# A hybrid attention layer with split fp32r products: mask, adaLN, second norm and tail loads rearranged

## The chip, the core and the metric

The kernel runs on one core of a Trainium2 chip. The core has a matrix engine (TensorE, PE), a vector engine (VectorE, DVE), a scalar engine (ScalarE, ACT), a small general engine (GpSimd, POOL) and a queue engine that issues transfers (SyncE, SP). Each runs its own instructions in order and waits for the others by semaphores. PE sums into PSUM, in banks of 512 f32 columns; everything else lies in SBUF. The metric is the device time of one execution in microseconds (us), lower is better.

## What is computed

One decoder layer for 256 tokens (T = 2 halves of 128) of width 2048, all in f32, weights 300 MB in all. The conditioning vector c gives six adaLN vectors of 2048. Cut to what matters here:

```python
mod = silu(c) @ w_ada + b_ada
shift_a, scale_a, gate_a, shift_f, scale_f, gate_f = split(mod, 6)
h = rms_norm(x, g_attn_pre) * (1 + scale_a) + shift_a
proj = h @ w_in                        # 8 differential heads, 8 sparse heads, 16 indexers
diff = softmax(q1 k1^T / 8, causal) - lam * softmax(q2 k2^T / 8, causal)   # per head, then @ v
sparse = softmax(q k^T / sqrt(128), only the 64 keys that the indexer picked)  # then @ v
mixed = concat(norm(diff @ v), sparse @ v) @ w_o
x = x + gate_a * rms_norm(mixed, g_attn_post)
h = rms_norm(x, g_ffn_pre) * (1 + scale_f) + shift_f
ff = (silu(h @ w_gate) * (h @ w_up)) @ w_down
x = x + gate_f * rms_norm(ff, g_ffn_post)
```

## The kernel before

**Products.** A full-precision product is made of three fp32r products of the halves of its operands (`mm3`: hi by hi L192, hi by lo L195, lo by hi L196). `wload` fetches a 1 MB piece of a weight (four k-slices of 512 columns) into one of six `raw` buffers; ACT rounds it to `whi` (L179) and DVE subtracts to get `wlo` (L180), in pieces of 128x1024 with three buffers each. Activations are kept as two halves of the same kind (`h`, `gT`, `mixT`, and `H2` for the FFN).

**adaLN.** `ada_block` makes a vector piece from w_ada, in units of 1 MB (four k-slices of 512 columns). With `on_pe` each slice is one product with c as the fixed operand, 32 columns wide, and four of these lie side by side on the array (L236, tile `ad`). Without it DVE does one multiply-add per slice into `aacc` (L244). `ada_cols` turns a finished row into columns of `modA` or `modF`, with two columns of `sel` for a PE block (L293) or with `ones` per accumulator for a DVE block (L297). modF (scale_f and shift_f) has four blocks of 512; F_DVE names those that DVE takes. Units are used one after the other by `ada_step`, which `side()` calls behind each w_o load and the FFN's first stage at a rate FRATE.

**Stages.** The input projection (about 35 to 390 us), with attention in steps among its products (to 440); w_o (to 503); FFN (508 to 1253); output. Three PSUM banks (`tr_bank`) serve all transposes, score products and small results, four (`mm_bank`) the large sums.

**Attention.** `to_T` transposes q and k (L410) and ACT copies them out (L413). `scores` (L490) puts two softmaxes into two banks, each with a 128-column segment (the first 128 queries) and a 256-column one. `softmax_parts` lets DVE scale, add the mask and take the row extreme in one custom step into SBUF (L501), and ACT takes exp from SBUF (L505). Then come the weighted sum, transposes (L513, L515) and the products with v.

**End of w_o.** `tail_pair` sums the last two column blocks (ci 2 and 3). All loads but the last two are used for both token halves at once. The last two (one per block, one of them in `xhi`/`xlo`) are used for t = 0 first and then for t = 1, 24 products each, so that `residual(0)` runs beside t = 1. `residual` squares the sum on ACT (L783), multiplies by Ga on DVE (L784), gets the row factor ry, makes x1 = x1 + y ry (L859), squares x1 on ACT (L861), gets its row factor r1 on POOL and dg, the diagonal matrix of r1 (L864). `h2_tiles` transposes x1 through dg on PE (L846), and `make_h` (L347 on ACT, L348 on DVE, L350) shifts, scales and splits it into `H2`; `first_half` does the first 8 of 16 k-slices.

**FFN.** With only those 8 slices made, the first NSPLIT column blocks of gate and up are half-summed and copied to `part` (L903), while `ada_step` gets the rest of modF; then the other 8 slices follow, and DVE adds the two halves. `tail_pair` ends w_down in the same manner as w_o, and `out_block` (L972) writes the output.

**Order.** The instructions of an engine are put in order by a scheduler at build time, which works from dependences and modelled times; `keep_in_program_order` pins a few. The order is fixed when the kernel runs.

```python
blocks = [(a, ci) for a in range(0, nk - 4, 4) for ci in cs]
...
tl = {ci: wload(rows, kbase + nk - 4, 4, ci * 512, 512, ph2 if ci == cs[1] else None)
      for ci in cs}
for t in range(T):
    for ci in cs:
        ...
    done[0](t)
```

## Time and profile before

| | before |
|---|---|
| three runs, us | 1262.14, 1262.45, 1264.23 |
| profiled execution, us | 1263.92 |
| its span, us | 1262.1 |
| PE busy | 1230.5 us (97%) |
| DVE busy | 763.6 us (60%) |
| ACT busy | 573.1 us (45%) |
| POOL busy | 23.2 us (2%) |
| HBM read | 307.05 MB |

The span runs from the first instruction to the last; 1.8 us of the profiled execution lie around it. Busy times of different engines lie beside one another and cannot be added. PE's records overlap one another, so a record's length is not what it costs: the distance between starts is. The chain of waits is followed back from the last instruction, and "idle ... <-X" names what released an instruction that had to wait.

### The profile page before, as it was taken

What the parts mean: (1) busy time and instruction counts of PE and PEld (TensorE: products, weight loads), DVE (VectorE), ACT (ScalarE), POOL (GpSimd) and SP (SyncE); (2) the same over time, 40 slices, a digit from 0 to 9 for tenths busy, and PEclk for the clock granted to TensorE, in tenths of its full rate; (3) what the DMA queues carried; (4) which work ended last, traced back from release to release, by engine and by line L of the source; (5) the groups of instructions that cost most, each with busy time, mean ns of one, the idle gap of its engine ahead of it and who ended that gap; (6) DMA issues with size and microseconds to landing.
All of it is one profiled execution on the core that took longest, in us unless ns stands there. A gap on an engine that the chain in (4) does not pass through costs nothing.

```text
span 1262.1 us, 15223 instructions
## 1 busy us (share of the span) xinstructions
PE 1230.5 (97%) x5912; PEld 948.6 (75%) x5912; DVE 763.6 (60%) x1155; ACT 573.1 (45%) x838; POOL 23.2 (2%) x63
## 2 busy tenths in 40 slices
PE   5999999999999999899999999999999999999997
PEld 4666675777656877788888888888888888888885
...
GB/s 382 388 358 334 371 357 204 370 258 272 200 304 266 150 366 279 267 190 322 314 278 262 179 192 241 255 172 195 199 177 192 200 191 185 193 198 182 185 134 67
DMA packets 44713, 310.14 MB, mean 246 GB/s; under 512 B 5848, under 2 KB 5848, under 8 KB 7648
## 3 DMA queue, kind: packets, MB, share of 16 engines
...
q10 hardware_dynamic: 272, 0.00, 0.0%
HBM read 307.05 MB, written 2.10 MB: 245 GB/s over the span
## 4 chain that ended last, share of the span: by engine, by line
PE 93%; DMA 2%; ACT 2%; DVE 1%; issue 1%; POOL 0%; SPq 0%; DVEq 0%; POOLq 0%
PE mm L195 27%; PE mm L192 27%; PE mm L196 27%; PE ad L236 5%; DMA raw<-in_w_ada_dram 1%; PE tr L490 1%; DMA raw<-in_w_in_dram 1%; PE tr L429 1%; PE tr L934 1%; PE tr L410 1%; PE tr L846 1%; PE tr L312 1%; DVE wlo L180 0%; PE tr L293 0%; PE tr L513 0%
## 5 line engine op out<-in xcount | busy, mean ns | idle before, releaser
L180 DVE TENSOR_TENSOR wlo<-raw,whi 128x1024 fp32r<-128x1024 f32 (+1 forms) x383 | 463.4, 1213 | 369.0 <-ACT whi L179 368.2
L179 ACT ACTIVATE whi<-raw 128x1024 fp32r<-128x1024 f32 (+1 forms) x383 | 401.0, 1051 | 519.5 <-PE mm L196 488.6
L195 PE MATMUL mm<-wlo,h 128*128 128x512 f32 (+1 forms) x1056 | 415.1, 393 | 0.8 <-DVE wlo L180 0.8
L196 PE MATMUL mm<-whi,h 128*128 128x512 f32 (+1 forms) x1056 | 410.9, 389 | 1.6 <-DVE h L350 1.6
L192 PE MATMUL mm<-whi,h 128*128 128x512 f32 (+1 forms) x1056 | 380.1, 393 | 1.9 <-ACT whi L179 1.0
L192 PEld LDWEIGHTS mm<-whi,h 128*128 128x128 f32 x1056 | 196.7, 188 | 63.3 <-issue 13.4
L195 PEld LDWEIGHTS mm<-wlo,h 128*128 128x128 f32 x1056 | 198.6, 188 | 60.3 <-issue 10.8
L196 PEld LDWEIGHTS mm<-whi,h 128*128 128x128 f32 x1056 | 198.6, 188 | 42.3 <-DVE h L350 2.1
L195 PE MATMUL mm<-wlo,gT 128*128 128x512 f32 x348 | 135.8, 390 | 0.0
L196 PE MATMUL mm<-whi,gT 128*128 128x512 f32 x348 | 135.4, 389 | 0.0
L192 PE MATMUL mm<-whi,gT 128*128 128x512 f32 x348 | 123.0, 390 | 0.0
L244 DVE SCALAR_TENSOR_TENSOR aacc<-raw,csil,aacc 128x512 f32<-128x512 f32 x126 | 94.0, 747 | 8.0 <-DMA raw<-in_w_ada_dram 5.3
L236 PE MATMUL ad<-raw,c 128*32 128x512 f32 (+2 forms) x640 | 82.8, 523 | 12.8 <-DMA raw<-in_w_ada_dram 12.8
L748 DVE TENSOR_TENSOR PR<-mm,PR 128x512 f32<-128x512 f32 (+1 forms) x88 | 57.0, 669 | 34.2 <-PE mm L196 34.0
L196 PEld LDWEIGHTS mm<-whi,gT 128*128 128x128 f32 x348 | 65.3, 188 | 13.9 <-issue 0.2
L195 PEld LDWEIGHTS mm<-wlo,gT 128*128 128x128 f32 x348 | 65.3, 188 | 13.6 <-issue 0.2
L192 PEld LDWEIGHTS mm<-whi,gT 128*128 128x128 f32 x348 | 65.3, 188 | 13.5
L195 PE MATMUL mm<-wlo,mixT 128*128 128x512 f32 x124 | 49.9, 402 | 0.0
L236 PEld LDWEIGHTS ad<-raw,c 128*32 128x32 f32 x640 | 17.9, 111 | 41.6 <-issue 26.7
L192 PE MATMUL mm<-whi,mixT 128*128 128x512 f32 x124 | 47.6, 402 | 0.7 <-ACT mixT L603 0.7
L196 PE MATMUL mm<-whi,mixT 128*128 128x512 f32 x124 | 45.9, 394 | 0.0
L195 PEld LDWEIGHTS mm<-wlo,mixT 128*128 128x128 f32 x124 | 23.3, 188 | 8.4 <-issue 1.7
(192 smaller groups left out, 673.2 us busy)
## 6 DMA issues: line engine op xcount, KB each, us to landing
raw<-in_w_ada_dram SPq DMA_DIRECT2D x96, 1024.0 KB, 7.2
raw<-in_w_gate_dram SPq DMA_DIRECT2D x44, 1024.0 KB, 5.0
raw<-in_w_up_dram SPq DMA_DIRECT2D x44, 1024.0 KB, 5.0
raw<-in_w_down_dram SPq DMA_DIRECT2D x44, 1024.0 KB, 4.9
raw<-in_w_in_dram SPq DMA_DIRECT2D x39, 1024.0 KB, 7.1
raw<-in_w_o_dram SPq DMA_DIRECT2D x16, 1024.0 KB, 7.0
xs<-in_x_dram SPq DMA_DIRECT2D x2, 1024.0 KB, 6.9
x<-in_x_dram SPq DMA_DIRECT2D x2, 1024.0 KB
```

The source lines that it names most:

```text
L179: made = [ACT.activation(hv, src, AF.Copy), DVE.tensor_tensor(lv, src, hv.bitcast(F32), op=ALU.subtract)]
L180: DVE.tensor_tensor(lv, src, hv.bitcast(F32), op=ALU.subtract)]
L192: i = PE.matmul(ps, lhsT=hi, rhs=whi, start=start, stop=False)
L195: PE.matmul(ps, lhsT=hi, rhs=wlo, start=False, stop=False)
L196: PE.matmul(ps, lhsT=lo, rhs=whi, start=False, stop=stop)
L236: PE.matmul(st["ps"][32 * j:32 * j + 32, :n], lhsT=c33[:, k, 1 - b:33 - b], rhs=w, start=(b == 0 and k < 4), stop=(b == nb - 1 and k >= 12 ...
L244: DVE.scalar_tensor_tensor(acc, w, csil[:, k:k + 1], acc, op0=ALU.mult, op1=ALU.add)
L312: PE.matmul(ps, lhsT=ones, rhs=accs[0], start=True, stop=True)
L410: PE.transpose(tr[:, i * P:(i + 1) * P], PR[:, t, c0:c0 + P], ident)
L429: PE.matmul(sc[i][:, SEG[t]], lhsT=st["q"][r, (2 * j + t) * P:(2 * j + t + 1) * P], rhs=ikT[r, :P * (t + 1)], start=True, stop=True)
L490: PE.matmul(sc[i][:, SEG[t]], lhsT=l, rhs=r, start=True, stop=True)
L748: DVE.tensor_tensor(dst, banks[c0][t][:, :n], dst, op=ALU.add)
```

## The change

Six things change.

1. The mask M is bf16, and so is nselb, the mask of picked keys. `score_banks` first multiplies an identity (`identb`) by the mask into the bank, 128x384, and the score products add to it. q is scaled when it is copied out of the transpose. DVE takes the negated row maximum straight from the bank, and ACT takes exp straight from the bank too.
2. F_DVE is (2, 3): the fourth block of modF goes to DVE.
3. Four column blocks of gate and up are half-summed instead of two (NSPLIT), with `ada_step` at half the rate (FRATE), and `side()` stops two units into modF's second half (SIDE). The partial sums lie in what y, Ga and xhi/xlo held; Gf is loaded and multiplied by its gate later.
4. `post_attn` and `residual` get the second norm from three means, of the square of the sum, of y x1, and of y squared (`st3`), with the mean square of x (`msx`): the mean square of the new x1 is msx + 2 ry mean(y x1) + ry^2 mean(y^2). x1 itself is no longer squared.
5. `tail_pair` keeps the last three loads instead of two for t = 0 and then t = 1, 36 products each, in w_o and in w_down; two of them lie in xhi/xlo and in the upper half of H2.
6. `h2_tiles` makes k-slices in pairs: one half of the pair from DVE, one from ACT, then one rounding copy and one subtraction for both.

```diff
-F_DVE = (2,)
+F_DVE = (2, 3)
...
-FRATE = 2
+FRATE = 1
...
-NSPLIT = 2
+NSPLIT = 4
+SIDE = 2
...
+    identb = ct([P, P], "identb", BF16)
+    DVE.tensor_copy(identb, ident)
+    M = ct([P, 384], "mask", BF16)
...
+    msx = ct([P, T], "msx")
+    DVE.tensor_scalar(msx, ssx, 1.0 / D, EPS, op0=ALU.mult, op1=ALU.add)
...
+        if ns:
+            ACT.activation(o[:, :ns * P], tr[:, :ns * P], AF.Copy, scale=scale)
+        if ns * P < n:
+            ACT.activation(o[:, ns * P:n], tr[:, ns * P:n], AF.Copy)
...
-    def scores(mms):
+    def score_banks(mask, mms):
 
         sc = [tr_bank() for _ in range(2)]
+        for i in range(2):
+            PE.matmul(sc[i][:, :384], lhsT=identb, rhs=mask, start=True, stop=False)
         for t in range(T):
             for i in range(2):
                 l, r = mms(i, t)
-                PE.matmul(sc[i][:, SEG[t]], lhsT=l, rhs=r, start=True, stop=True)
+                PE.matmul(sc[i][:, SEG[t]], lhsT=l, rhs=r, start=False, stop=(t == T - 1))
...
-                DVE.tensor_tensor_reduce(out=s[:, i, SEG[t]], in0=sc[i][:, SEG[t]], in1=mask[:, SEG[t]],
-                                         scale=-scale, scalar=2.0 ** 120, op0=ALU.add, op1=ALU.min,
-                                         accum_out=mn[:, i, t:t + 1])
+                DVE.tensor_reduce(mx[:, i, t:t + 1], sc[i][:, SEG[t]], axis=AX.X, op=ALU.max,
+                                  negate=True)
             for t in range(T):
-                ACT.activation(s[:, i, SEG[t]], s[:, i, SEG[t]], AF.Exp, scale=-1.0,
-                               bias=mn[:, i, t:t + 1], accum_out=l[:, i, t:t + 1])
+                ACT.activation(s[:, i, SEG[t]], sc[i][:, SEG[t]], AF.Exp, bias=mx[:, i, t:t + 1],
+                               accum_out=l[:, i, t:t + 1])
...
+            st["q"] = to_T([(0, c0), (1, c0), (0, c0 + P), (1, c0 + P)], 128 ** -0.5, 4)
...
+    def post_attn(bank, t, ci):
+
+
+        cs_ = slice(ci * 512, ci * 512 + 512)
+        j = tr_bank()
+        ACT.activation(j, bank, AF.Square, scale=D ** -0.5, accum_out=st3[:, t, 0, ci:ci + 1])
+        DVE.tensor_tensor(y[:, t, cs_], bank, Ga[:, cs_], op=ALU.mult)
+        j2 = ph2.tile([P, 512], F32, tag="sil", name=nm("j2"), bufs=3)
+        DVE.tensor_tensor_reduce(out=j2, in0=y[:, t, cs_], in1=x1[:, t, cs_], scale=2.0 / D, scalar=0.0,
+                                 op0=ALU.mult, op1=ALU.add, accum_out=st3[:, t, 1, ci:ci + 1])
+        ACT.activation(j, y[:, t, cs_], AF.Square, scale=D ** -0.5, accum_out=st3[:, t, 2, ci:ci + 1])
...
-        blocks = [(a, ci) for a in range(0, nk - 4, 4) for ci in cs]
-        for a, ci in blocks:
+        blocks = [(a, ci) for a in range(0, nk, 4) for ci in cs]
+        for a, ci in blocks[:-3]:
             for (k, _), (whi, wlo) in wload(rows, kbase + a, 4, ci * 512, 512).items():
                 for t in range(T):
                     mm3(banks[ci, t], *L(k - kbase), t, whi, wlo, k == kbase, False)
             side()
-        tl = {ci: wload(rows, kbase + nk - 4, 4, ci * 512, 512, ph2 if ci == cs[1] else None)
-              for ci in cs}
+
+        spare = [tuple(ph2.tile([P, 1024], F32R, tag=tag, name=nm(tag)) for tag in ("xhi", "xlo"))]
+        spare += [tuple(H2[:, i, k:k + 4, :].rearrange("p k q -> p (k q)") for i in range(2)) for k in (8, 12)]
+        homes = (None, (None, spare[0]), spare[1:])
+        tl = [(ci, wload(rows, kbase + a, 4, ci * 512, 512, homes[i])) for i, (a, ci) in enumerate(blocks[-3:])]
         for t in range(T):
-            for ci in cs:
-                for (k, _), (whi, wlo) in tl[ci].items():
+            for ci, ws in tl:
...
+        if used[0] < need_f1 + SIDE:
+            ada_step(1)
...
+            for i in range(0, 4, 2):
+                hf = wp.tile([P, S], F32, tag="hf", name=nm("hf"), bufs=2)
+                for j in range(2):
+                    src, kk = tr[:, (i + j) * P:(i + j + 1) * P], k + i + j
+                    sc, sh = modF[:, 1, kk:kk + 1], modF[:, 0, kk:kk + 1]
+                    if j:
+                        ACT.activation(hf[:, P:], src, AF.Identity, bias=sh, scale=sc)
+                    else:
+                        DVE.tensor_scalar(hf[:, :P], src, sc, sh, op0=ALU.mult, op1=ALU.add)
+                hi, lo = (H2[:, h, k + i:k + i + 2, qs] for h in range(2))
+                hv = hf.rearrange("p (k q) -> p k q", k=2)
+                ACT.activation(hi, hv, AF.Copy)
+                DVE.tensor_tensor(lo, hv, hi.bitcast(F32), op=ALU.subtract)
...
-            post(banks[ci, t], t, ci, Ga, ssy, y)
-        DVE.tensor_reduce(sst[:, t:t + 1], ssy[:, t], axis=AX.X, op=ALU.add)
-        rstd(ry[:, t:t + 1], sst[:, t:t + 1], 1, D)
+            post_attn(banks[ci, t], t, ci)
+        DVE.tensor_reduce(mean[:, t], st3[:, t], axis=AX.X, op=ALU.add)
+        rt = ry[:, t:t + 1]
+        POOL.tensor_tensor(rt, mean[:, t, 0:1], nhalf[:, 0:1], op=ALU.pow)
+        m = mean[:, t, 1:2]
+        DVE.scalar_tensor_tensor(m, mean[:, t, 2:3], rt, m, op0=ALU.mult, op1=ALU.add)
+        tc.keep_in_program_order(
+            DVE.scalar_tensor_tensor(m, m, rt, msx[:, t:t + 1], op0=ALU.mult, op1=ALU.add))
+        POOL.tensor_tensor(r1[:, t:t + 1], m, nhalf[:, 0:1], op=ALU.pow)
+        POOL.tensor_scalar(dg[t], ident, r1[:, t:t + 1], None, op0=ALU.mult)
         for h in range(2):
             hs = slice(1024 * h, 1024 * h + 1024)
-            DVE.scalar_tensor_tensor(x1[:, t, hs], y[:, t, hs], ry[:, t:t + 1], x1[:, t, hs],
-                                     op0=ALU.mult, op1=ALU.add)
-            ACT.activation(y[:, t, hs], x1[:, t, hs], AF.Square, accum_out=ss1[:, t, h:h + 1])
-        POOL.tensor_tensor(sss[:, t:t + 1], ss1[:, t, 0:1], ss1[:, t, 1:2], op=ALU.add)
-        rstd(r1[:, t:t + 1], sss[:, t:t + 1], 1, D, POOL)
-        POOL.tensor_scalar(dg[t], ident, r1[:, t:t + 1], None, op0=ALU.mult)
+            tc.keep_in_program_order(
+                DVE.scalar_tensor_tensor(x1[:, t, hs], y[:, t, hs], rt, x1[:, t, hs], op0=ALU.mult, op1=ALU.add))
...
+            part = ph2.tile([P, 8, 512], F32, tag="y", name="part")
+            part2 = big.tile([P, 4, 512], F32, tag="Ga", name="part2")
+            part3 = [ph2.tile([P, T, 512], F32, tag=tag, name="part3" + tag) for tag in ("xhi", "xlo")]
+
+            def part_of(lc, wi, t):
+                if lc < 2:
+                    return part[:, 4 * lc + 2 * wi + t, :]
+                if lc == 2:
+                    return part2[:, 2 * wi + t, :]
+                return part3[wi][:, t, :]
...
+            if fc == NSPLIT - 1:
+                Gf = big.tile([P, D], F32, tag="Ga", name="Gf")
+                tc.keep_in_program_order(SP.dma_start(Gf, g_ffn_post[0].partition_broadcast(P)))
+                for b in range(4):
+                    ada_gate(Gf, 5, b * 512, False)
```

On PE in attention, at the second pair of sparse heads (`tr` are the shared PSUM banks, `skT` and `qT` transposed keys and queries, `s` the weighted probabilities, `on` a differential head's output). Before:

```order
L513 MATMUL tr_3286<-ident,s_3188 128x128
L490 MATMUL tr_3292<-skT,qT_3204 128x128
L490 MATMUL tr_3293<-skT,qT_3204 128x128
L490 MATMUL tr_3292<-skT,qT_3204 128x256
L490 MATMUL tr_3293<-skT,qT_3204 128x256
L513 MATMUL tr_3286<-ident,s_3188 128x128 x2
L410 MATMUL tr_3309<-ident,PR 128x128 x4
L602 MATMUL tr_3362<-ident,on_3269 128x128 x2
```

After:

```order
L527 MATMUL tr_3318<-ident,s_3220 128x128
L502 LDWEIGHTS identb
L502 MATMUL tr_3324<-nselb,identb 128x384
L502 LDWEIGHTS identb
L502 MATMUL tr_3325<-nselb,identb 128x384
L506 MATMUL tr_3324<-skT,qT_3236 128x128
L506 MATMUL tr_3325<-skT,qT_3236 128x128
L506 MATMUL tr_3324<-skT,qT_3236 128x256
L506 MATMUL tr_3325<-skT,qT_3236 128x256
L527 MATMUL tr_3318<-ident,s_3220 128x128 x2
L421 MATMUL tr_3343<-ident,PR 128x128 x4
L617 MATMUL tr_3395<-ident,on_3301 128x128 x2
```

Two products of the mask with their weight loads now stand ahead of the score products; the rows behind them are the same.

On PE at the end of w_o (`mm_3876` and `mm_3920` are the last sums, of token half 1; `dg` products make the transposed x1; `ad` is adaLN). Before:

```order
L192 MATMUL mm_3876<-xhi_4146,mixT_1559 128x512
L195 MATMUL mm_3876<-xlo_4147,mixT_1559 128x512
L196 MATMUL mm_3876<-xhi_4146,mixT_1560 128x512
L236 MATMUL ad_4123<-raw_4366,c_105 32x512 x4
L236 MATMUL ad_4123<-raw_4372,c_105 32x512 x4
L236 MATMUL ad_4123<-raw_4412,c_105 32x512 x4
L236 MATMUL ad_4123<-raw_4418,c_105 32x512 x4
L846 MATMUL tr_4236<-dg_3871,x_3850 128x128 x4
L846 MATMUL tr_4257<-dg_3871,x_3850 128x128 x4
L192 MATMUL mm_4326<-whi_4330,h_3866 128x512
```

After:

```order
L195 MATMUL mm_3920<-h_3911,mixT_1567 128x512
L198 MATMUL mm_3920<-h_3911,mixT_1567 128x512
L199 MATMUL mm_3920<-h_3911,mixT_1568 128x512
L877 MATMUL tr_4229<-dg_3915,x_3883 128x128 x4
L877 MATMUL tr_4244<-dg_3915,x_3883 128x128 x4
L195 MATMUL mm_4296<-whi_4300,h_3911 128x512
L198 MATMUL mm_4296<-wlo_4301,h_3911 128x512
```

The sixteen adaLN products between the last w_o product and the dg products are gone. The last products of half 1 read weights from H2's place.

On DVE at the same place (`wlo_4331` and `wlo_4301` are the first FFN weights). Before:

```order
L180 TENSOR_TENSOR wlo_4143<-raw_4140,whi_4142 128x1024
L784 TENSOR_TENSOR y<-mm_3873,Ga 128x512
L784 TENSOR_TENSOR y<-mm_3875,Ga 128x512
L855 TENSOR_REDUCE sst<-ssy 128x1
L155 TENSOR_SCALAR rs_4181<-sst 128x1
L859 SCALAR_TENSOR_TENSOR x_3850<-y,ry,x_3850 128x1024 x2
L180 TENSOR_TENSOR wlo_4331<-raw_4328,whi_4330 128x1024
L784 TENSOR_TENSOR y<-mm_3874,Ga 128x512
```

After (ISA with `j` and `st` is the summed product of y and x1, the next ISA reads its sum out):

```order
L247 SCALAR_TENSOR_TENSOR aacc_4416<-raw_4421,csil,aacc_4416 128x512
L806 TENSOR_TENSOR y<-mm_3919,Ga 128x512
L247 SCALAR_TENSOR_TENSOR aacc_4416<-raw_4421,csil,aacc_4416 128x512
L808 ISA j_4162,st_121<-y,x_3883 128x512
L808 ISA st_121 128x1
L183 TENSOR_TENSOR wlo_4301<-raw_4298,whi_4300 128x1024
L897 TENSOR_REDUCE mean<-st_121 128x3
L183 TENSOR_TENSOR wlo_4305<-raw_4298,whi_4304 128x1024
L901 SCALAR_TENSOR_TENSOR mean<-mean,ry 128x1
L183 TENSOR_TENSOR wlo_4341<-raw_4338,whi_4340 128x1024
L903 SCALAR_TENSOR_TENSOR mean<-mean,ry,msx 128x1
L909 SCALAR_TENSOR_TENSOR x_3883<-y,ry,x_3883 128x1024 x2
```

Between half 0's sums and its x1 stand adaLN multiply-adds and three wlo steps, where before only the norm's own steps stood.

## Rows read from the trace of the kernel before

**Rows 1.** The page: share of the chain that ended last, by engine.

```profile
PE 93%; DMA 2%; ACT 2%; DVE 1%; issue 1%; POOL 0%; SPq 0%; DVEq 0%; POOLq 0%
```

**Rows 2.** Stretches of 50 us: length, then busy us (instructions) per engine, clock, DMA.

```profile
400.00:450.00 50.00, 46.83 (x260) 38.94 (x259) 32.21 (x75) 33.91 (x89) 2.73 (x4) 1.00 0.53 188
...
1000.00:1050.00 50.00, 50.00 (x222) 41.40 (x221) 24.46 (x22) 20.03 (x19) 0.00 (x0) 1.00 0.56 191
```

**Rows 3.** Timeline of PE in the FFN: start us, length us.

```profile
599.62 0.39 PE L192 MATMUL mm<-whi,h 128*128 128x512 f32 x1
599.85 0.39 PE L195 MATMUL mm<-wlo,h 128*128 128x512 f32 x1
```

**Rows 4.** adaLN: PE's groups by shape, then two steps of the chain.

```profile
L236 PE MATMUL ad<-raw,c 128*32 128x512 f32 x448 | 73.0, 603 | 0.0
...
470.12 0.98 PE ad L236 x2
...
521.27 0.79 PE tr L293 x8
```

**Rows 5.** Small products: timeline of a 336-column sum, and a plain f32 group.

```profile
64.75 0.32 PE L195 MATMUL mm<-wlo,h 128*128 128x336 f32 x1
64.90 0.32 PE L196 MATMUL mm<-whi,h 128*128 128x336 f32 x1
...
L312 PE MATMUL tr<-aacc,ones 128*128 128x512 f32 x16 | 8.2, 592 | 0.0
```

**Rows 6.** Softmax steps of DVE and ACT by shape, and one stretch.

```profile
L501 DVE CUSTOM_DVE_ANT_0 s<-tr,mask 128x256 f32<-128x256 f32 x16 | 6.7, 418 | 0.0
...
L505 ACT ACTIVATE s<-s,mx 128x256 f32<-128x256 f32 x24 | 11.9, 497 | 0.0
...
L505 ACT ACTIVATE s<-s,mx 128x128 f32<-128x128 f32 x24 | 9.5, 396 | 10.2 <-DVE mx L501 10.2
...
405.00:415.00 10.00, 8.36 (x49) 6.72 (x50) 8.29 (x27) 7.92 (x30) 1.39 (x2) 1.00 0.82 288
```

**Rows 7.** Timeline of PE at the end of w_o.

```profile
503.31 3.64 PE L236 MATMUL ad<-raw,c 128*32 128x512 f32 x32
508.25 2.05 PE L846 MATMUL tr<-dg,x 128*128 128x128 f32 x16 [1.30 <-POOL dg L864]
...
512.41 0.50 PE L196 MATMUL mm<-whi,h 128*128 128x512 f32 x1 [1.65 <-DVE h L350]
513.84 0.79 PE L192 MATMUL mm<-whi,h 128*128 128x512 f32 x1 [0.93 <-ACT h L345]
514.43 0.63 PE L195 MATMUL mm<-wlo,h 128*128 128x512 f32 x1
514.86 0.63 PE L196 MATMUL mm<-whi,h 128*128 128x512 f32 x1
```

**Rows 8.** The stretch of 10 us around it.

```profile
510.00:520.00 10.00, 7.43 (x35) 5.84 (x34) 5.83 (x16) 7.27 (x19) 1.67 (x4) 0.83 1.01 427
```

**Rows 9.** Timelines of DVE, ACT and POOL at the end of w_o.

```profile
498.70 0.69 DVE L784 TENSOR_TENSOR y<-mm,Ga 128x512 f32<-128x512 f32 x1 [4.43 <-ACT tr L783]
...
502.70 1.22 DVE L180 TENSOR_TENSOR wlo<-raw,whi 128x1024 fp32r<-128x1024 f32 x1
...
502.23 1.05 ACT L861 ACTIVATE y<-x 128x1024 f32<-128x1024 f32 x1
...
507.58 0.62 POOL L864 TENSOR_SCALAR dg<-ident,r 128x128 f32<-128x128 f32 x1
```

**Rows 10.** A stretch behind the half-summed blocks of before.

```profile
590.00:600.00 10.00, 10.00 (x50) 8.38 (x49) 9.89 (x13) 4.65 (x7) 0.00 (x0) 1.00 0.88 313
```

**Rows 11.** Timeline of DVE at the end.

```profile
1252.73 0.74 DVE L972 SCALAR_TENSOR_TENSOR ff<-mm,ry,x 128x512 f32<-128x512 f32 x1
```

**Rows 12.** DMA issues: count, size, median us from issue to landing.

```profile
raw<-in_w_o_dram SPq DMA_DIRECT2D x16, 1024.0 KB, 7.0
...
Gf<-in_g_ffn_post_dram SPq DMA_DIRECT2D x1, 1024.0 KB, 14.6
```

More of the change, by code (lines that the diff above doesn't have):

```diff
@@ L169, in wload @@
                 w = min(step, n - b)
-                if more is not None and a + m == nk:
-                    hi = more.tile([P, 1024], F32R, tag="xhi", name=nm("xhi"))
-                    lo = more.tile([P, 1024], F32R, tag="xlo", name=nm("xlo"))
+                home = more[a // 2] if more else None
+                if home is not None:
+                    hi, lo = home
                 else:
@@ L389, in layer @@
     nsel = pp.tile([P, 384], F32, tag="nsel", name="nsel")
+    nselb = pp.tile([P, 384], BF16, tag="nselb", name="nselb")
     iwS = pp.tile([P, T, 16], F32, tag="iwS", name="iwS")
@@ L476, in tail @@
             DVE.tensor_tensor(nsel, nsel, score, op=ALU.is_equal)
-            DVE.tensor_scalar(nsel, nsel, NEG, None, op0=ALU.mult)
+            DVE.tensor_scalar(nselb, nsel, NEG, None, op0=ALU.mult)
         return [head] + [lambda r=r: rounds(r) for r in range(0, TOPK // 8, 2)] + [tail]
@@ L523, in s0 @@
         def s0():
[L524 removed]
+            st["q"] = to_T([(0, c0), (1, c0), (0, c0 + P), (1, c0 + P)], 128 ** -0.5, 4)
         def s1():
             qT = st["q"]
[L528 to L529 removed]
+            sc = score_banks(nselb, lambda i, t: (qT[:, (2 * i + t) * P:(2 * i + t + 1) * P],
+                                                  skT[:, :P * (t + 1)]))
+            st["s"], st["l"] = softmax_parts(sc)
         def s2():
@@ L847, in h2_tiles @@
                           rhs=dg[t], start=True, stop=True)
-            for i in range(4):
-                make_h(H2, tr[:, i * P:(i + 1) * P], modF, k + i, slice(t * P, (t + 1) * P),
-                       on_act=i % 2 == 1)
+            for i in range(0, 4, 2):
[11 more added lines that the diff above has]
+                DVE.tensor_tensor(lo, hv, hi.bitcast(F32), op=ALU.subtract)
@@ L906, in layer @@
                 h2_tiles(t, 8, 16)
-            for b in range(4):
-                ada_gate(Gf, 5, b * 512, False)
         for lc in range(ng):
+            if fc == NSPLIT - 1:
[3 more added lines that the diff above has]
+                    ada_gate(Gf, 5, b * 512, False)
             c0 = fc * 512
```

39 lines of the change are left out of this document (16 added, 23 removed).

## The prediction

> **What bounds the kernel now.** I read the page's chain of waits first: 93% of the chain that ended last is TensorE (PE) itself [rows 1]. So a change here is worth what it adds to or takes from PE's own queue, plus what it does to the few places where PE stands. The stretches of 50 us say where those are: the FFN shows 50.00 of 50 in every row, at clock 1.00; attention lacks 3.2 us in 400 to 450 [rows 2]. The PE timeline gives the true price of a product: a 128x512 record is 0.39 us long, but the next starts 0.23 us later (0.2265 over many) [rows 3]. All sums below go by such starts. In the FFN the number of products is unchanged and VectorE (DVE) and ScalarE (ACT) have slack [rows 2], so nothing is to be had there but the adaLN products. Three things are left: adaLN products, mask products, and the seam between w_o and the FFN.
>
> **1. The fourth quarter of modF leaves PE.** The 512-column adaLN products hold PE for 73.0 us in 448 records [rows 4], two records to a product: 224 products. F_DVE = (2, 3) makes that 192. Four neighbours run at once on four column tiles, so what costs is the run, not the product: a run of 2 records takes 0.98 us, as one of 8 does [rows 4]. Counting runs in the two orders (one run is up to four products in a row) gives 71 before and 59 after. The block's own work before is five short runs (some 0.98 each, 4.9) and one long one of 3.64 us just behind w_o [rows 7]: 8.6 us. The other three runs go because the rows that stay are cut up less. 12 x 0.98 = **-11.8 us**; at least -8.6, at most -12.5 (a change-over saved with some of them).
> What takes its place: DVE gets 30 more multiply-adds of 128x512 in the half-summed FFN blocks, where PE's products need only the raw weights' two halves. With one unit per two weight steps I lay out some 75 us of DVE work in the 87 us of those blocks. Before, the stage after the first two blocks had DVE at 9.89 of 10 us and PE at 10.00 of 10 [rows 10]: that load is hidden, so I take **0**. If the cover were gone, the overhang would be of the order of those 9 to 12 us (rival E). The block's finish costs 8 more tiny products with ones and 4 fewer with sel; eight records with sel take 0.79 us [rows 4]: **+0.6**, from +0.3 to +1.
>
> **2. Mask by product, exp out of PSUM.** 24 products of 128x384 in bf16 come in (16 with M, 8 with nselb), each with its own weight load. The trace has no bf16 product. From below: a 336-column fp32r product starts 0.15 us after the one before it [rows 5], so 384 columns at that pace are 0.177. From above: a product in plain f32 is two records, and 16 records of 512 columns held PE for 8.2 us [rows 5], 0.51 each; two of 384 columns are at most 0.77. The fp32r row is nearest, since it too goes through once; with some change-over, 0.20 each: 24 x 0.20 = **+4.8**, from +3.7 to +18. The Trainium skill ("TensorE: Matmul & The Clock Gate", Part 1) measures bf16 products at columns / 2.4 GHz plus 2.5 ns; by that, an estimate, the term would be 24 x 0.1625 = 3.9.
> The custom add-and-min on DVE (0.418 us for 256 columns [rows 6]) becomes a maximum of about that size: nothing on PE's path. What does move is when the bank comes free. Before, it was free when DVE had read it; now it is free only when ACT has done both exps from it, 0.50 + 0.40 = 0.9 us later [rows 6]. Three banks serve all transposes and scores. In the order, nine or ten places hand a bank from the scores to a transpose within a few rows (the DSA pairs and the last differential heads); elsewhere 4 or more long products stand between. Attention already lacks 1.64 us of 10 at 405 to 415 [rows 6]. I take two full holds exposed, **+2**, from 0 to +6. The Trainium skill ("PSUM — Partial Sum Buffer", "PSUM bank collisions raise a hardware error") wants two engines kept off one bank at once, reads included; it speaks against this part, since the maximum and the exp now share a bank. By that rule the first exp waits for both maxima and each hold grows by up to 0.42, so two holds would make 2.6 instead of 2.
>
> **3. The seam.** Before: after the last w_o product PE does 3.64 us of adaLN, then stands 1.30 us for dg, 1.65 and 0.93 us for the h pieces, with two short slots between, and then runs at 0.43 us a product instead of 0.23 [rows 7]: the granted clock was 0.83 over 510 to 520 [rows 8], some 3.4 us at the lower level (1.2 GHz) after those idle stretches. Idle 3.9, slow products about 1.2, change-overs and slow transposes 0.8: 5.9 us lost.
> After: the last three loads instead of two close the sums, so token half 1 has 36 products behind half 0, 8.15 us instead of 5.44 (24). The adaLN run is gone. In its place the norm of half 0 has no longer to wait for x1: four squares (1.05 us each [rows 9]) and the sum of two go. Its chain is square, y, product with x1, square of y, mean, power, two tiny steps, power, dg. With 0.69 for y and as much for the product, under 0.8 for a square (that of twice the columns took 1.05), 0.62 for dg and about as much for a power [rows 9], and 0.5 for the tiny steps, that is some 5.3 us; but DVE runs in order, and four adaLN steps and three wlo (1.22 each [rows 9]) stand among them. Laid out by hand, dg is ready 8.1 to 8.25 us after half 0's last product, PE is free after 8.15 to 8.2: idle 0.25. The second four transposes wait for bank and ACT, 1.6, then the first h pieces, 0.9: 2.75 us in all. That gives 2.75 - 5.9 = **-3.2**; from -5.9 (no idle) to +2 (one 1.22 us step late at each of three waits, and the lower clock again).
> About the clock: the Trainium skill (same page, Part 1) states that the slow state is the default and that idling brings it back. The trace agrees at 513 to 517 us, but shows 1.00 in attention in spite of idle there [rows 2]. If it falls again after the seam, the price by these rows is some 1.7 us (1256.0); I give that 3 in 10 inside the forecast.
>
> **4. The rest.** Eight more half-sum copies on ACT and eight adds on DVE lie under 50.00 of 50 PE us: 0. h2 in pairs saves small steps, counted in 3. Loading Gf later: 0. At the end, the old tail has DVE still in the first half's output at 1252.73, for 0.74 us [rows 11], when the last sum is due; with 36 products for half 1, that work and the other column block's are done earlier: **-0.6**, from 0 to -0.9.
>
> **Sum.** -11.8 + 0.6 + 4.8 + 2 - 3.2 - 0.6 = **-8.2 us**. The profiled execution is 1263.92 (span 1262.1 and 1.8 around it), 1.5 above the median; against it the sum gives 1255.7, against the median of 1262.45 it gives **1254.3**. Its own range, from the likelier halves of the bounds, is 1249 to 1259.
>
> **Rivals.**
> D, better: the seam closes wholly (-5.9 instead of -3.2) and no bank hold shows (0 instead of +2): -12.9, **1249.5**. For it: DVE has less to do in attention. Against: the DVE queue at the seam is still full.
> B, the banks give it back: the nine or ten close places each expose a hold of 0.9, +8.6 instead of +2: -1.6, **1260.9**, no change that can be told. For it: PE is in order, so a transpose that waits for its bank holds the w_o products behind it; 405 to 415 shows such waits already [rows 6]. Against: the 3.2 us that 400 to 450 lacks are there with the old hold, which was DVE's own two steps long, and ACT has had slack.
> E, the quarter only changes its place: DVE falls behind in the half-summed blocks, PE waits for wlo, and 8 us come back: **1262.3**; this is the case in which the change does not do what it says. Against it: [rows 10], a heavier load with PE at 10.00.
> C, slower: a late load at the seam. The order puts two adaLN units (aacc of raw_4376 and raw_4421) on DVE ahead of w_o's last wlo and of y, so DVE stands until they land, and PE and the norm behind it. Loads of 1 MB landed in 7.0 us (w_o), but Gf's in 14.6 [rows 12], just in this stretch, where the DMA share was 1.01 [rows 8]. At the latter DVE comes 7.6 us late, all of it on PE, with 3.4 us at the lower clock after it (+1.7), and dg's chain again out of cover (+2): -8.2 + 11.3 = +3.1, **1265.5**. It is slower from a landing of about 14 us on, and hardly shows below 7. Against it: the fourth quarter's PE loads no longer stand in w_o.
>
> **How the numbers follow.** Forecast 0.55, D 0.12, B 0.13, E 0.09, C 0.11. 0.2%, 2.5 us, is about what a measurement of this kernel can tell from no change. Faster holds the forecast (all but 0.02), D and a third of B: 0.69. Same holds most of B, E and that 0.02: 0.19. Slower holds C and the mask at its upper price: 0.12. The range reaches from the lower bounds of 1 to 3 together (-12.5 + 3.7 - 5.9 with 0.5 for the rest, 1247.5) to past E, 1263; C and the tip of D are left out.
>
> **What would show it.** The 512-column adaLN group at 384 records and some 62 us; 24 identb products that start about 0.2 us ahead of their score products; behind the last w_o product no adaLN run, an idle of under 0.5 before the dg products and under 3 in all, and the clock of 510 to 520 at 1.00; PE at 50.00 of 50 from 520 to 620 with DVE near 43; PE lacking 5 to 6 us in 400 to 450 instead of 3.2, the new waits released by the exp. I am wrong if PE waits for wlo in the half-summed blocks, if waits on the exp come to over 6 us, or if DVE stands for an adaLN load just before y.

## The result and the profile after

The changed kernel took 1256.43 us (median of 6 runs, 1255.14 to 1256.97), the kernel before 1264.27 beside it (6 runs): ratio 0.994, 95% interval 0.9928 to 0.9953, or 7.8 us less. 8.2 less had been forecast, which was 1254.3 as counted from the three runs then known. A second set of runs of the changed kernel gave 1254.91 (1253.17 to 1256.56), ratio 0.9929 (0.9916 to 0.9942). The profiled execution is 1256.72, its span 1254.9 against 1262.1.

**The products.** PE's groups by shape in the changed kernel; the 512-column adaLN group answers to [rows 4]. The other three are the mask products with M, the products with ones (16 before), and the mask products with nselb.

```profile
L239 PE MATMUL ad<-raw,c 128*32 128x512 f32 x384 | 61.1, 603 | 0.0
...
L502 PE MATMUL tr<-mask,identb 128*128 128x384 bf16 x16 | 5.0, 332 | 0.0
...
L300 PE MATMUL tr<-ones,aacc 128*128 128x1 f32 x32 | 3.9, 231 | 0.0
...
L502 PE MATMUL tr<-nselb,identb 128*128 128x384 bf16 x8 | 2.5, 330 | 0.0
```

448 adaLN records became 384, and 73.0 us busy became 61.1, as forecast. How PE's whole time moved is seen by adding up, over all of PE's records, the distance from each start to the next (a wait of over 0.1 us is counted as idle):

| PE, from its first product to its last | before | after | difference |
|---|---|---|---|
| adaLN products (L236, now L239) | 78.29 | 66.94 | -11.35 |
| finishes with ones and sel | 7.30 | 8.11 | +0.81 |
| mask products (24) | 0 | 4.61 | +4.61 |
| transposes of s (L513, now L527) and score products | 23.21 | 20.51 | -2.70 |
| w_in, w_o and FFN products | 1065.07 | 1066.20 | +1.13 |
| idle | 10.27 | 11.59 | +1.32 |
| all others | | | +0.26 |
| sum | | | -5.92 |

PE began 0.7 us earlier and what follows its last product is 0.56 shorter: -7.2, the difference of the spans. The earlier start is no part of the gain: the kernel before with F_DVE alone changed (below) began 0.4 earlier too.

**The half-summed blocks.** Two stretches of 50 us, the second just behind these blocks: PE is full, and DVE is at 31 of 50. The quarter of modF that DVE took over costs PE nothing there.

```profile
550.00:600.00 50.00, 50.00 (x239) 41.77 (x238) 30.68 (x41) 27.17 (x40) 0.99 (x2) 1.00 0.69 247
600.00:650.00 50.00, 50.00 (x226) 41.49 (x225) 30.79 (x33) 24.90 (x28) 0.00 (x0) 1.00 0.54 188
```

**Attention.** The stretch that answers to the first of [rows 2], and PE's two waits there on the exp (who waits, for whom: us in total, times, longest).

```profile
400.00:450.00 50.00, 47.20 (x258) 38.71 (x257) 29.27 (x55) 32.89 (x84) 2.75 (x4) 0.97 0.53 192
...
PE tr L617 <- ACT s L519: 0.5, 1, 0.5
...
PE tr L600 <- ACT s L519: 0.4, 1, 0.4
```

PE lacks 2.8 us in it where it lacked 3.2. Only 0.9 us are waits on the exp; the old wait on DVE's row extreme is gone.

**The seam.** PE's timeline, which answers to [rows 7]; then DVE's and GpSimd's (POOL), which answer to [rows 9].

```profile
485.01 0.50 PE L198 MATMUL mm<-wlo,mixT 128*128 128x512 f32 x1 [1.20 <-DVE wlo L183]
...
498.32 0.39 PE L199 MATMUL mm<-h,mixT 128*128 128x512 f32 x1
500.76 2.05 PE L877 MATMUL tr<-dg,x 128*128 128x128 f32 x16 [2.06 <-POOL dg L905]
503.37 0.50 PE L195 MATMUL mm<-whi,h 128*128 128x512 f32 x1 [0.55 <-ACT h L890]
...
504.38 0.50 PE L199 MATMUL mm<-whi,h 128*128 128x512 f32 x1 [0.28 <-DVE h L891]
...
508.39 2.05 PE L877 MATMUL tr<-dg,x 128*128 128x128 f32 x16 [0.99 <-POOL dg L905]
```

```profile
488.40 0.75 DVE L247 SCALAR_TENSOR_TENSOR aacc<-raw,csil,aacc 128x512 f32<-128x512 f32 x1 [2.00 <-DMA raw<-in_w_ada_dram]
...
494.70 1.21 DVE L183 TENSOR_TENSOR wlo<-raw,whi 128x1024 fp32r<-128x1024 f32 x1
496.35 0.22 DVE L901 SCALAR_TENSOR_TENSOR mean<-mean,ry 128x1 f32<-128x1 f32 x1 [0.44 <-POOL ry L899]
496.49 1.22 DVE L183 TENSOR_TENSOR wlo<-raw,whi 128x1024 fp32r<-128x1024 f32 x1
...
497.75 2.48 DVE L909 SCALAR_TENSOR_TENSOR x<-y,ry,x 128x1024 f32<-128x1024 f32 x2
```

```profile
494.86 1.46 POOL L899 TENSOR_TENSOR ry<-mean,nhalf 128x1 f32<-128x1 f32 x1 [83.37 <-DVE mean L897]
497.92 1.53 POOL L904 TENSOR_TENSOR r<-mean,nhalf 128x1 f32<-128x1 f32 x1 [1.60 <-DVE mean L903]
499.54 1.17 POOL L905 TENSOR_SCALAR dg<-ident,r 128x128 f32<-128x128 f32 x1
```

Behind the last w_o product (498.32) there is no adaLN run any more, but PE idles 2.06 us for dg, 0.55, 0.28 and 0.99: 3.88 in all, just what 1.30, 1.65 and 0.93 made before. But no product ran at the lower clock here. From the last w_o product to the end of the second sixteen dg products, less 0.2265 for each product, 1.8 for sixteen transposes and the adaLN run, 6.0 us were lost before and 4.9 now. Earlier, at 485.01, PE stood 1.20 us for wlo. DVE stood 2.00 us for an adaLN load ahead of half 0's y (488.40). And look at GpSimd: the two powers took 1.46 and 1.53 us, dg 1.17. Before, with DVE idle beside it, dg took 0.62 [rows 9].

**The end.** DVE's timeline: the first half's output is done before the last sum (1246.43) is due, unlike in [rows 11].

```profile
1242.12 1.41 DVE L1028 SCALAR_TENSOR_TENSOR ff<-mm,ry,x 128x512 f32<-128x512 f32 x2
...
1246.43 0.69 DVE L794 TENSOR_TENSOR ff<-mm,ff 128x512 f32<-128x512 f32 x1 [1.29 <-PE mm L199]
```

### The profile page after: what moved, and what is told of

It is laid out like the page before. It is cut to its first block, busy times and chain, and to the rows that moved or that the text cites. A ratio compares the mean times of both kernels' runs of the same rounds, so it can differ in the third digit from the quotient of the medians.

```text
span 1254.9 us, 15182 instructions
## 1 busy us (share of the span) xinstructions
PE 1223.2 (97%) x5880; PEld 950.1 (76%) x5880; DVE 791.3 (63%) x1151; ACT 574.5 (46%) x845; POOL 25.4 (2%) x61
## 4 chain that ended last, share of the span: by engine, by line
PE 58%; issue 1%; DVE 0%; ACT 0%; DVEq 0%; POOLq 0%; POOL 0%
PE mm L198 19%; PE mm L199 19%; PE mm L195 19%; PE tr L990 1%; PE tr L877 0%; PE tr L315 0%; PE tr L300 0%; DVE ff L1028 0%; ACT tr L797 0%; DVE ff L794 0%; DVEq L1064 0%; POOLq L1064 0%; POOL ry L159 0%; DVE sst L1037 0%; DVE rs L158 0%
## 5 line engine op out<-in xcount | busy, mean ns | idle before, releaser
L183 DVE TENSOR_TENSOR wlo<-raw,whi 128x1024 fp32r<-128x1024 f32 (+1 forms) x379 | 458.1, 1213 | 323.0 <-ACT whi L182 322.6
L182 ACT ACTIVATE whi<-raw 128x1024 fp32r<-128x1024 f32 (+1 forms) x379 | 396.9, 1051 | 496.0 <-PE mm L199 463.1
L198 PE MATMUL mm<-wlo,gT 128*128 128x512 f32 x340 | 132.7, 390 | 0.0
L199 PE MATMUL mm<-whi,gT 128*128 128x512 f32 x340 | 132.3, 389 | 0.0
L247 DVE SCALAR_TENSOR_TENSOR aacc<-raw,csil,aacc 128x512 f32<-128x512 f32 x156 | 116.3, 747 | 16.8 <-DMA raw<-in_w_ada_dram 14.0
L195 PE MATMUL mm<-whi,gT 128*128 128x512 f32 x340 | 120.0, 390 | 0.0
L239 PE MATMUL ad<-raw,c 128*32 128x512 f32 (+2 forms) x576 | 71.0, 514 | 12.0 <-DMA raw<-in_w_ada_dram 12.0
L199 PEld LDWEIGHTS mm<-whi,gT 128*128 128x128 f32 x340 | 63.8, 188 | 13.4 <-issue 0.2
L195 PEld LDWEIGHTS mm<-whi,gT 128*128 128x128 f32 x340 | 63.8, 188 | 13.3
L198 PE MATMUL mm<-wlo,mixT 128*128 128x512 f32 x116 | 46.5, 401 | 1.2 <-DVE wlo L183 1.2
L195 PE MATMUL mm<-whi,mixT 128*128 128x512 f32 x116 | 45.2, 407 | 0.4 <-ACT mixT L564 0.4
L199 PE MATMUL mm<-whi,mixT 128*128 128x512 f32 x116 | 42.9, 395 | 0.0
L239 PEld LDWEIGHTS ad<-raw,c 128*32 128x32 f32 x576 | 15.7, 111 | 35.7 <-issue 21.6
```

What stands on the lines that cost most here:

```text
L182: made = [ACT.activation(hv, src, AF.Copy), DVE.tensor_tensor(lv, src, hv.bitcast(F32), op=ALU.subtract)]
L183: DVE.tensor_tensor(lv, src, hv.bitcast(F32), op=ALU.subtract)]
L195: i = PE.matmul(ps, lhsT=hi, rhs=whi, start=start, stop=False)
L198: PE.matmul(ps, lhsT=hi, rhs=wlo, start=False, stop=False)
L199: PE.matmul(ps, lhsT=lo, rhs=whi, start=False, stop=stop)
L239: PE.matmul(st["ps"][32 * j:32 * j + 32, :n], lhsT=c33[:, k, 1 - b:33 - b], rhs=w, start=(b == 0 and k < 4), stop=(b == nb - 1 and k >= 12 ...
```

## The experiments

Each kernel is the changed one with the edit shown, unless the text says otherwise; times are medians beside the kernel before (1263.94 to 1264.33).

### Old softmax put back

```diff
-            PE.matmul(sc[i][:, :384], lhsT=identb, rhs=mask, start=True, stop=False)
...
+                DVE.tensor_tensor_reduce(out=s[:, i, SEG[t]], in0=sc[i][:, SEG[t]], in1=mask[:, SEG[t]],
```

> The changed kernel with the softmax of the kernel before alone put back (mask added and row extreme taken by DVE, exp from SBUF, no identb products). By the prediction's terms the identb products (4.8 us) and the bank holds (2 us) go: about 1249.6. By the slots of the two traces the identb products took 4.6 us, but the transposes and score products around them took 2.7 us less than before, so only 1.9 of that is net, and the waits on the exp (0.9) and the 3 us at the lower clock in attention (1.2) may go with it: 1252 to 1253. Rival: where the banks come free costs nothing and the products are hidden, then it stays at 1256.

Measured: 1254.61 (ratio 0.9932, 0.9919 to 0.9944). Against 1256.43 that looks like a price of 1.8 us for the mask part; against the second set of the changed kernel (1254.91) it is nothing.

### No mask at all

```diff
-        for i in range(2):
-            PE.matmul(sc[i][:, :384], lhsT=identb, rhs=mask, start=True, stop=False)
...
-                PE.matmul(sc[i][:, SEG[t]], lhsT=l, rhs=r, start=False, stop=(t == T - 1))
+                PE.matmul(sc[i][:, SEG[t]], lhsT=l, rhs=r, start=True, stop=True)
```

> The changed kernel without any mask in the attention scores (causal and picked keys both left out), all else as it is: maximum and exp still come out of PSUM. It parts the price of the products from the price of the longer bank hold: against the changed kernel the products go, and the kernel with the old softmax put back (1254.6) differs from it by the hold alone. If the products cost what their neighbours don't give back, 1.9 us, it is 1254.5 and the hold costs nothing; if they cost their full 4.6, it is 1251.8 and exp out of PSUM is itself a gain of 2.8 over the old softmax; if the hold is what costs, it stays above 1255.5.

Measured: 1253.3 (0.9922, 0.991 to 0.9934), 1.6 to 3.1 below the changed kernel, so near the net price of the products or between it and the full one. It is 1.3 below the old softmax, with overlapping intervals. That speaks against a bank hold that costs; the times don't show a gain by exp out of PSUM. The trace does show something: added up as in the table, the transposes of s and the score products took 21.2 us in this kernel, 20.5 in the changed one and 23.2 with the old softmax. So 2.0 of their 2.7 us go with the new softmax and its order, and not with the mask products.

### The fourth block back on PE

```diff
-F_DVE = (2, 3)
+F_DVE = (2,)
```

> The changed kernel with the fourth block of modF alone given back to PE. The slots of the two traces put 11.35 us on these products and give 0.8 us back at the block's finish: 1266 to 1267. Rival: the DVE steps and the adaLN loads at the seam (DVE stood 4.0 us for loads between 470 and 490, PE 1.2 us for wlo and 2.06 for dg) belong to this block, so that much comes back and it is only 1262 to 1264.

Measured: 1268.41 (1.0039, 1.0026 to 1.0052): 12.0 to 13.5 above the changed kernel. The whole gain and more hangs on this block: without it the other parts make the kernel 4.5 us slower than the kernel before. The rival that the seam gives part of it back falls by the time. Its waits are there: in this trace PE idles 2.2 us less than in the changed kernel. But the adaLN products take 12.9 us more there, not 11.35, and the rest of PE's work and the end some 2 more.

### The fourth block alone

The kernel before, with this edit and no other:

```diff
-F_DVE = (2,)
+F_DVE = (2, 3)
```

> The kernel before with the fourth block of modF on DVE and nothing else changed. PE's own time falls by 10.5 us (11.35 less 0.8 at the finish); but the long run of 3.64 us behind w_o was cover for the chain to dg, and goes with it, so PE idles that much more: 1264 - 10.5 + 3.6 = 1257. If this is right, the other parts of the change together bring about 1 us. Rivals: DVE's 30 more steps do not fit under two half-summed blocks and w_o: 1262 or above; or the cover is not missed: 1253.5.

Measured: 1265.26 (1.0008, 0.9999 to 1.0017): no gain at all. My 1257 was wrong by 8 us. First PE at the seam, then the stretch of 10 us ahead of dg (with clock), then DVE in the norm of half 0:

```profile
506.45 3.78 PE L846 MATMUL tr<-dg,x 128*128 128x128 f32 x16 [8.28 <-POOL dg L864]
...
500.00:510.00 10.00, 3.55 (x17) 3.55 (x17) 9.54 (x13) 3.73 (x8) 2.80 (x5) 0.67 0.96 384
...
492.08 2.08 DVE L244 SCALAR_TENSOR_TENSOR aacc<-raw,csil,aacc 128x512 f32<-128x512 f32 x3
...
494.67 0.15 DVE L855 TENSOR_REDUCE sst<-ssy 128x1 f32<-128x4 f32 x1
494.74 1.41 DVE L244 SCALAR_TENSOR_TENSOR aacc<-raw,csil,aacc 128x512 f32<-128x512 f32 x2
496.06 0.15 DVE L155 TENSOR_SCALAR rs<-sst 128x1 f32<-128x1 f32 x1
```

PE idles 8.28 us for dg instead of 1.30, and the granted clock is 0.67 in this stretch. I had counted only the lost cover of 3.64. But the adaLN steps that DVE now has were put by the scheduler between the norm's own steps (aacc between y and the mean, and between the mean and what follows), so the chain from half 0's last product to dg also became longer, 13.8 us instead of 10.4. So the block pays only together with the rest of the change; the next runs show in part what of it counts.

### Two resident loads

```diff
-        blocks = [(a, ci) for a in range(0, nk, 4) for ci in cs]
-        for a, ci in blocks[:-3]:
+        blocks = [(a, ci) for a in range(0, nk - 4, 4) for ci in cs]
+        for a, ci in blocks:
```

> The changed kernel with two resident loads instead of three at the end of w_o and of w_down. Half 1 gives 2.7 us less cover for the chain to dg, which is 2.06 us late already: 2.7 more of idle at the seam, and 0.6 at the end: 1259.5 to 1260. Rival: the order moves other products into the gap, and only the 0.6 shows: 1257.

Measured: 1259.83 (0.9971, 0.996 to 0.9981), 3.4 to 4.9 more. PE at the seam:

```profile
504.04 3.79 PE L875 MATMUL tr<-dg,x 128*128 128x128 f32 x16 [6.08 <-POOL dg L903]
```

Idle 6.08 instead of 2.06 or, in the second profile of the changed kernel, 3.04; and the 16 products behind it take 3.79 us instead of 2.05, at the lower clock. Of the parts undone here the third load weighs most beside the block. But without it the kernel is still 4.1 us faster than the kernel before, so it is not all that makes the block's move pay.

### Old second norm

```diff
-        DVE.tensor_reduce(mean[:, t], st3[:, t], axis=AX.X, op=ALU.add)
...
+            ACT.activation(y[:, t, hs], x1[:, t, hs], AF.Square, accum_out=ss1[:, t, h:h + 1])
+        POOL.tensor_tensor(sss[:, t:t + 1], ss1[:, t, 0:1], ss1[:, t, 1:2], op=ALU.add)
```

> The changed kernel with the second norm alone as before (squares of x1 on ACT, mean square from it). The chain to dg gets x1's two steps and two squares of 1.05 us in it again, about 3 us for half 0, and 1 to 2 us for half 1: 1259 to 1261. Rival: dg is late by GpSimd's slow steps, not by the length of the chain, and the old chain has as many GpSimd steps, which then meet other DVE work: within 1 us of 1256.4.

Measured: 1256.07 (0.9945, 0.9932 to 0.9958): no difference that can be told. GpSimd's second power and dg with the old norm, the DVE step beside them, and PE's longest wait behind dg:

```profile
495.60 1.38 DVE L799 TENSOR_TENSOR y<-mm,Ga 128x512 f32<-128x512 f32 x2
...
496.11 0.55 POOL L159 TENSOR_TENSOR r<-rs,nhalf 128x1 f32<-128x1 f32 x1
496.76 0.61 POOL L907 TENSOR_SCALAR dg<-ident,r 128x128 f32<-128x128 f32 x1
...
502.45 0.50 PE L195 MATMUL mm<-whi,h 128*128 128x512 f32 x1 [2.97 <-ACT h L892]
```

The power takes 0.55 us and dg 0.61. The old chain has them after x1; the step that DVE then does takes one of its inputs from PSUM (mm), and does not hold them up. The new chain is two squares shorter, but has its second power and dg beside x1's steps, where they take 0.98 and 0.56 longer. So dg comes no earlier by the new chain: 10.3 and 11.3 us behind half 0's last product in the two profiles of the changed kernel, 10.2 with the old norm. The old norm loses some of it again in the h pieces (2.97).

### dg on ACT

```diff
-        POOL.tensor_scalar(dg[t], ident, r1[:, t:t + 1], None, op0=ALU.mult)
+        ACT.activation(dg[t], ident, AF.Copy, scale=r1[:, t:t + 1])
```

> The changed kernel with dg made on ACT instead of GpSimd. The trace shows dg's step at 1.17 us on GpSimd beside x1's steps on DVE (0.62 before, with DVE idle); ACT needs under 0.4 and waits for nothing there. dg comes 0.8 to 0.9 earlier for each half, PE's 2.06 and 0.99 of idle shrink by that: 1254.6 to 1255.4. Rival: x1 or the shared banks bind there too, and it stays at 1256.4.

Measured: 1252.95 (0.992, 0.9908 to 0.9932), less than the 1254.6 expected, the fastest kernel of the study with the whole computation, 2.0 below the second set of the changed kernel and 3.5 below the first. The intervals overlap a little, so it is faster than the kernel before, and probably than the changed one. PE at the seam:

```profile
497.55 1.16 PE L877 MATMUL tr<-dg,x 128*128 128x128 f32 x8 [1.92 <-ACT dg L905]
499.26 1.16 PE L877 MATMUL tr<-dg,x 128*128 128x128 f32 x8 [0.55 <-ACT tr L810]
```

dg's own step took 0.40 us. PE's idle at the seam is 2.9 us instead of 3.9 or, in the second profile, 3.6; and no fall of the clock shows in this execution from 16 us to PE's last product. What is left are the two slow powers and the steps and waits of DVE around them, 2.91 us for the load among them.

### Old softmax, dg on ACT, x1 in steps of 512

```diff
-        for h in range(2):
-            hs = slice(1024 * h, 1024 * h + 1024)
+        for h in range(4):
+            hs = slice(512 * h, 512 * h + 512)
```

> Old softmax, dg on ACT, and x1 made in four steps of 512 columns for each half instead of two of 1024. If the price of the mask part (1.0 to 1.8 us) and of dg (2.6 to 3.5) add up, and the second power gets its turn after 0.65 us of DVE instead of 1.25, then 1250.5 to 1251.5, faster than both kernels. By the theory of the shared way of GpSimd and DVE to SBUF the second power of each half is then about 0.9 to 1.0 us long instead of 1.53. Rival: the order at the seam that the old softmax gets (dg idle of 2.95) eats it: 1253.

Measured: 1254.84 (0.9929, 0.9917 to 0.9942), 3.3 above the 1251.5 that the two prices would give: they don't add. The 1.9 above dg on ACT alone is too little to tell. But the second power behaved as the theory of a shared way said:

```profile
496.29 0.99 POOL L900 TENSOR_TENSOR r<-mean,nhalf 128x1 f32<-128x1 f32 x1 [1.60 <-DVE mean L899]
...
503.53 0.99 POOL L900 TENSOR_TENSOR r<-mean,nhalf 128x1 f32<-128x1 f32 x1 [0.80 <-DVE mean L899]
```

0.99 for both halves, against 1.53 with steps of 1024. It ends about 0.4 to 0.5 us behind the end of the DVE step that runs when it starts, be that step 0.74 or 1.28 us long.

### Two half-summed blocks

```diff
-NSPLIT = 4
+NSPLIT = 2
-FRATE = 1
+FRATE = 2
```

> The changed kernel with two half-summed blocks instead of four and adaLN steps at the old rate of two; the fourth block of modF stays on DVE. The half-summed stage is then some 44 us long instead of 87, and the units of the fourth block and the wlo steps (some 75 us of DVE work in the changed kernel) no longer fit under it: PE waits for wlo or for modF, 10 us or more: 1266 to 1272. Rival: DVE's work spreads to w_o and to later blocks, and only small waits show: 1257 to 1259.

Measured: 1257.42 (0.9956, 0.9941 to 0.997). The rival was right: DVE was full, and only small waits show. The stretch 580 to 600, and PE's waits for whi in the whole execution (us in total, times, longest):

```profile
580.00:600.00 20.00, 20.00 (x94) 16.62 (x94) 20.00 (x26) 9.45 (x11) 0.00 (x0) 1.00 0.85 317
...
PE mm L195 <- ACT whi L182: 3.3, 2, 2.0
```

The longer of the two, 1.98 us at 534.5, lies in the half-summed blocks. Four blocks instead of two bring at most 2.5 us.

### adaLN steps kept away from the seam, in two ways

A later start in the half-summed blocks:

```diff
-                        if used[0] < need_f2:
-                            ada_step(min(FRATE, need_f2 - used[0]))
+                        if lc and used[0] < need_f2:
+                            ada_step(min(2 if lc < 3 else 1, need_f2 - used[0]))
```

> The changed kernel with the adaLN steps of the half-summed blocks starting one block later (none in the first, two per step in the second and third), so that the scheduler finds fewer of them to put at the seam. The loads that DVE stood for there (4.0 us in all, PE 1.2 us for wlo behind them) should go: 1254.5 to 1255.5. Rival: the same DVE time comes back as PE waits in the half-summed blocks or at the second half of modF: 1256.4 or above.

Measured: 1261.18 (0.9981, 0.9972 to 0.9989). DVE's first y of half 0 now waited for ACT and not for a load. But the scheduler put later units at the seam instead, and dg came 3.74 us late; its own step took 2.35 us on GpSimd, beside x1, an aacc step and the product of y and x1:

```profile
485.67 0.69 DVE L806 TENSOR_TENSOR y<-mm,Ga 128x512 f32<-128x512 f32 x1 [3.84 <-ACT tr L805]
...
497.13 2.35 POOL L905 TENSOR_SCALAR dg<-ident,r 128x128 f32<-128x128 f32 x1
```

Program order for these steps, with dg on ACT:

```diff
+                    if pin_dve[0]:
+                        tc.keep_in_program_order(i_)
```

> The kernel with dg on ACT, with the DVE steps of the adaLN units that are called in the half-summed blocks held in program order, behind x1's steps at the seam. DVE then does not stand at the seam for a 1 MB load (2.9 us before y in the trace with dg on ACT), and dg comes earlier by up to that: PE's idle of 1.92 there goes to under 0.5, time 1251 to 1251.5. Rival: the 13 units moved fill DVE in the half-summed blocks, and PE waits for wlo or for modF's second half there: 1253 or above.

Measured: 1260.16 (0.9972, 0.9961 to 0.9983). Here too DVE stood for no load ahead of y. PE waited 2.53 us for dg, so more than the 1.92 with dg on ACT, and in the half-summed blocks for whi:

```profile
524.02 1.22 PE L195 MATMUL mm<-whi,h 128*128 128x512 f32 x2 [3.14 <-ACT whi L182]
...
526.30 0.63 PE L195 MATMUL mm<-whi,h 128*128 128x512 f32 x1
526.73 0.63 PE L198 MATMUL mm<-wlo,h 128*128 128x512 f32 x1
```

Behind the idle of 3.14 us the products ran at the lower clock (0.43 us from start to start). Both edits took the wait for the load off DVE, and neither made dg early: it came 12.0 and 10.8 us behind half 0's last product. With two half-summed blocks, where DVE had no such wait either, it was 9.7. So the wait is a part of the lateness and not its main cause. What it costs at y can be read off: the last y of half 0 starts 0.9 to 1.0 us behind half 0's last product in these three traces, 1.2 and 2.2 in the two profiles of the changed kernel.

### The changed kernel again

> The changed kernel again, unaltered, beside the others of this call. Its 6 runs gave 1256.43 (1255.14 to 1256.97), and its profiled run fell to the lower clock twice (about 30 to 40 and 405 to 415 us) where the kernel with dg on ACT, the same up to w_o's end, did not and was 3.2 us ahead there. If that was chance of the runs, this gives 1254.5 to 1257 again with a spread over 2 us; if it comes to 1253, the 3.5 us of dg on ACT was mostly a difference between calls.

Measured: 1254.91, spread 3.4 us. DVE's wait for the load and PE's for dg in this profile:

```profile
485.97 0.75 DVE L247 SCALAR_TENSOR_TENSOR aacc<-raw,csil,aacc 128x512 f32<-128x512 f32 x1 [3.04 <-DMA raw<-in_w_ada_dram]
...
498.33 2.68 PE L877 MATMUL tr<-dg,x 128*128 128x128 f32 x16 [3.04 <-POOL dg L905]
```

Both are 1.0 us longer than in the first profile. The loss at the seam is 5.9 us here, against 4.9 there. The stretches where the clock fell, in the first profile and in this one:

```profile
30.00:40.00 10.00, 8.34 (x60) 5.67 (x49) 4.43 (x5) 7.08 (x12) 0.00 (x0) 0.83 1.01 413
405.00:415.00 10.00, 8.91 (x44) 7.06 (x42) 6.72 (x17) 6.96 (x25) 1.37 (x2) 0.83 0.86 317
...
495.00:505.00 10.00, 7.11 (x38) 5.43 (x37) 8.92 (x19) 5.31 (x14) 4.69 (x4) 1.00 0.50 196
```

```profile
30.00:40.00 10.00, 8.67 (x76) 5.72 (x72) 4.70 (x7) 8.32 (x14) 0.00 (x0) 1.00 1.01 414
405.00:415.00 10.00, 8.21 (x50) 6.53 (x50) 5.74 (x15) 7.83 (x31) 1.37 (x2) 1.00 0.77 301
...
495.00:505.00 10.00, 6.96 (x31) 5.41 (x30) 9.36 (x20) 4.65 (x12) 5.16 (x5) 0.83 0.23 93
```

The same kernel fell to the lower level at 30 to 40 and at 405 to 415 us in one execution, at 495 to 505 in the other. Eight products or so at 0.43 us instead of 0.23 make some 1.6 us for each fall, an estimate; shorter waits take up a part of it. Counted at the same products, the second execution was 1.3 us ahead behind the head, 1.9 behind attention and 3.4 at w_o's end (1.2 of it the wait at 485.01). Hence differences of under 2 us between the kernels here can't be told.

Change 6 (k-slices in pairs) and SIDE had no run of their own.

## Why the prediction came true, and where its steps were wrong

**The fourth block: right.** 12 runs at 0.98 were -11.8; the ledger has -11.35. The finish was +0.6 and is +0.81. Nothing came back in the half-summed blocks (rival E).

**The mask: 5 us too dear.** The product itself was right: 0.20 forecast, 4.61 / 24 = 0.192 measured. (By the Trainium skill, "TensorE: Matmul & The Clock Gate", Part 1, an estimate of 0.1625; the measurement decides.) Two terms failed. The score products and the transposes about them, for which the sum had no term, took 2.70 us less, so +1.9 is the net; 2.0 of that stays without the mask products, so it comes with the new softmax. By which of its steps no run shows. The bank hold was to cost 2; the waits on the exp are 0.9, and about as much of the old waits went, so 0. Rival B is out. No run shows that keeping the two engines apart at one bank cost anything.

**The seam: -1.1 in one profile and -0.1 in the other instead of -3.2.** dg was to be 0.25 late and was 2.06 late in one profile, 3.04 in the other. PE was free 8.2 us behind half 0's last product, as laid out. But dg came 10.3 and 11.3 us behind it instead of 8.1 to 8.25, and had come 10.4 behind it before: the chain became no shorter. What was mis-sized is GpSimd: some 0.62 for each power and for dg, from a row where DVE was idle. With DVE's steps beside them they took 1.46, 1.53 and 1.17: 2.3 us more, 2.0 of it on the chain (DVE stood 0.44 behind the first power). That is about the whole lateness in the first profile; the 1.0 more in the second goes with DVE's longer wait for the load. The trace before already had the answer, in GpSimd's timeline there: the first step ran beside wlo, the second, the same for half 1, with DVE idle.

```profile
505.80 1.04 POOL L155 TENSOR_SCALAR rs<-sss 128x1 f32<-128x1 f32 x1
...
513.26 0.19 POOL L155 TENSOR_SCALAR rs<-sss 128x1 f32<-128x1 f32 x1
```

I had quoted only a fast step. The Trainium skill ("SBUF — State Buffer", "SBUF: two separate sides") says that GpSimd and DVE share one pair of ways to SBUF as an exclusive lock, held for the whole step when DVE reads two SBUF inputs and GpSimd reads SBUF too. The traces agree: powers of 0.55 alone, 0.99 and 1.53 beside steps of 0.74 and 1.28; and a memset, which reads nothing, ran on unhindered beside wlo. GpSimd and DVE in the changed kernel in attention:

```profile
257.03 0.53 POOL L222 MEMSET aacc<- 128x512 f32 x1 [53.26 <-PE tr L315]
...
256.49 1.22 DVE L183 TENSOR_TENSOR wlo<-raw,whi 128x1024 fp32r<-128x1024 f32 x1
```

**Rival C was half there.** DVE did stand for adaLN loads ahead of y (2.00 us), and PE 1.20 for wlo behind them, with loads of about 7 us, not 14.6. That was priced at "hardly shows below 7".

**The clock.** The 3 in 10 for a fall at the seam was the right kind of thought at too few places: in the two profiles it fell at the head, in attention and at the seam. The Trainium skill ("TensorE: Matmul & The Clock Gate", Part 1) lets idling bring the slow state back. The traces show idle in such places in every execution, and a fall in some.

**The end: right**, -0.56 for -0.6; with two resident loads, as undone above, it is 0.6 longer again.

So the sum of -8.2 met the measured -7.8 by luck. The mask was 4.9 too dear. Against that stand, in the first profile, 2.1 that the seam did not give, 0.7 at the block, 1.2 of waiting for wlo, and some 2 of clock falls at the head and in attention. And the forecast did not see that its largest term depends on the rest of the change, of what was undone on the third resident load most: alone it is worth nothing.
